# Dense experts of layer 0: the low parts of u, and of the spilled v, made by VectorE instead of GpSimd

## The chip, the cores and the metric

One core of one Trainium2 chip runs the whole program as a single launch. The metric is the device time in microseconds (us), from the start of the execution to its end. Five engines run their own queues of instructions in order: TensorE (PE; its weight loads are PEld), VectorE (DVE), ScalarE (ACT), GpSimd (POOL) and SyncE (SP), which here only issues DMA transfers.

## The reference

Two layers of a backbone, each with a token mixer and then an expert network. The change lies in the expert network of layer 0:

```python
def _peer(h, w_q, sub_k1, sub_k2, u, v):
    ...                                   # top 16 experts of each of 8 heads, of 16384: idx, gate
    def block(args):
        hb, ib, gb = args
        act = jax.nn.gelu(jnp.einsum('td,ted->te', hb, u[ib])) * gb
        return jnp.einsum('te,ted->td', act, v[ib])
```

`h` has 512 tokens of 1024 features in layer 0 (256 of context, 256 latent). `u` and `v` have 16384 rows of 1024 numbers each.

## The kernel before

The 512 tokens of layer 0 are treated in two ways. The first 128 take the **gathered** path: for each of their 128 expert places, one row of `u` and later one of `v` is fetched per token by an indirect DMA from GpSimd's queue (tile `row`, 5 buffers, 512 KB each) and used by one VectorE instruction (L1045 for a row of u, whose partial result goes to `score`; L1063 for a row of v, added to `tok`). Rows of the modulation weights (`in_w_modT`, loaded by SyncE, used by L1035) stand in the same ring. One step of the generator `gathered` (`next(work)`) uses one row and issues the fetch of the one four places on.

The other 384 tokens take the **dense** path: all 16384 experts are computed, 128 slabs of 128 experts, two slabs to a group. For a group TensorE computes the scores S = u·h (L223, 48 matmuls with 384 columns), ScalarE applies gelu into `ga` (L1108), VectorE multiplies by the gate grid (L1253), and TensorE adds the product with v into `pa` (L1306, 36 matmuls with 512 columns).

Each fp32 operand is used as a high part and a low part, so that three products stand for one. `split` makes them: ScalarE rounds the slab to the high part (`wH` of u, `vH` of v, L210), and another engine subtracts, low = raw − high (`wL`, `vL`, L214). The factor `ga` gets the parts `ah` (ScalarE, L1256) and `al` (VectorE, L1260).

18 groups (36 slabs) have their scores computed before the dense loop and are **spilled** to DRAM (`spd`); the loop first takes the 46 unspilled groups, then the 18 spilled ones, which need only their v slabs and the stored `ga`. The tables that name the engine of the low part are `LOWU` (u slabs that are spilled), `LOWV` (v slabs, one string for the unspilled and one for the spilled groups), and a literal `"g"` for the u slabs of the loop.

The order on TensorE, VectorE, ScalarE and GpSimd in this loop is that of the code (a manual schedule). In turn g the code issues the loads of v for g+1, the scores of g+1, and then the 36 matmuls of `pa` of g, in eight parts numbered d; between the parts stand: d=0 the split of u for g+2, d=1 the gating of g+1, d=4 its `al`, d=5 the split of v for g+1 (d=0 in the spilled groups), and the steps of `gathered`: one at d=0, one at d=4 and four at d=7 in the unspilled groups; one at d=5 and one at d=7 in the spilled ones. The raw slabs of u and v share one ring of four buffers (`wraw`), loaded by SyncE's queue in order. With v two slabs and u two slabs alternating, a load of u(g+2) waits for the buffers that `vL` of g has read, and a load of v waits for those that `wL` has read.

Of the kernel before, what the change touches and what calls it, by code (L numbers as in the profile page):

```python
# [66 lines left out]
SPX = ((0, 2), (0, 0))  # L67
LOWQ = ('g', 'g')
LOWU = ('g', 'g')
LOWV = (("vv", "gg"), ("vv", "vv"))  # L70
GATED = (1, 4)
VALUES = (5, 0)
USTAGE = 0
# [110 lines left out]
class Kernel:  # L184
# [891 lines left out]
    def peer(self, l, mods, todo=()):  # L1076
        nc, A, tc = self.nc, self.A, self.tc
# [9 lines left out]
        with ExitStack() as es:  # L1087
# [7 lines left out]
            def low(s):  # L1095
                return tuple({"g": "gpsimd", "v": "vector"}[x] for x in s)

            def u_load(i, spilling=False):
                return [self.w_slab(A["uT"][l, i + e], "scalar", low(LOWU[l] if spilling else "g")) for e in range(2)]

            def u_pair(ws):

# [8 lines left out]
            def spill(upto):  # L1111

                while self.spilled < min(upto, nsp):
                    i = self.spilled
                    self.spilled += 2
                    nc.sync.dma_start(sp_d[i:i + 2].rearrange("i j t -> j i t"), u_pair(u_load(i, True)))
# [93 lines left out]
            with ExitStack() as e2:  # L1210
# [13 lines left out]
                def u_stage(g):  # L1224

                    if g >= len(order):
                        return
                    i = order[g]
                    if i >= nsp:
                        b.u[g] = u_load(i)  # L1230
                    else:
                        b.ga[g] = self.t(cp, [P, 2, n], tag="ga", bufs=3)
                        nc.sync.dma_start(b.ga[g], sp_d[i:i + 2].rearrange("i j t -> j i t"))
# [28 lines left out]
                def values(g):  # L1262
                    b.vs = [self.split(vp, w, "v", 4, low={"v": "vector", "g": "gpsimd"}[LOWV[l][order[g] < nsp][e]])
                            for e, w in enumerate(b.w)]
# [197 lines left out]
```

## Time and profile before

| | before |
|---|---|
| median of 3 runs (lowest, highest) | 2970.75 us (2959.99, 2982.71) |
| the profiled execution: time, span | 2970.65 us, 2968.9 us |
| TensorE busy | 2736.3 us (92%) |
| VectorE busy | 2122.4 us (71%) |
| ScalarE busy | 1141.9 us (38%) |
| GpSimd busy | 1452.2 us (49%) |
| DMA, mean over the span | 215 GB/s |

The busy times are means over stages that have little in common. The dense loop of layer 0 runs from about 782 to 1784 us of the span, the unspilled groups to about 1635 us. Matmuls are pipelined, so a busy TensorE need not be one at its peak.

### The profile page before, as it was taken

How to read it: one execution, taken by the hardware profiler on the slowest of the kernel's cores; microseconds unless marked ns; L12 is line 12 of the kernel's file. 1: busy time of each engine (PE TensorE's matmuls, PEld its weight loads, DVE VectorE, ACT ScalarE, POOL GpSimd, SP SyncE). 2: the span in 40 equal slices, each digit the busy share in tenths (PEclk: the TensorE clock that was granted, in tenths of full speed). 3: DMA queues.
4: the chain of work that ended last, by engine and by line, in shares of the span. 5: the costliest groups of instructions: out<-in, count | busy, mean ns of one | idle time of the engine just before them, and what ended most of it. 6: DMA issues, size and time to landing. Idle time of an engine off the chain costs nothing.

```text
span 2968.9 us, 41568 instructions
## 1 busy us (share of the span) xinstructions
PE 2736.3 (92%) x15750; PEld 2417.1 (81%) x15750; DVE 2122.4 (71%) x3488; ACT 1141.9 (38%) x1742; POOL 1452.2 (49%) x779
## 2 busy tenths in 40 slices
PE   7799999889999899989998998899889999999998
PEld 4677888889988888878887776678889998887776
DVE  6894778998587787888877887846894225566665
ACT  4333343335432332323333333344344544444443
POOL 3530144455377666667765883524655665440000
PEclk9898999999999999999999998999999999999999
DMA  6321423356787878888888982423557777667784
GB/s 230 107 93 60 127 89 110 101 195 257 271 315 278 302 279 297 304 296 318 309 298 311 338 273 85 142 64 116 160 160 252 241 255 225 189 190 260 271 277 167
DMA packets 265784, 639.24 MB, mean 215 GB/s; under 512 B 19184, under 2 KB 136688, under 8 KB 262768
## 3 DMA queue, kind: packets, MB, share of 16 engines
q1 hardware_dynamic: 228720, 502.36, 50.4%
q0 software_dynamic: 36864, 134.23, 12.3%
q8 instruction: 123, 2.02, 0.3%
q14 instruction: 77, 0.63, 0.1%
HBM read 574.39 MB, written 62.13 MB: 214 GB/s over the span
## 4 chain that ended last, share of the span: by engine, by line
PE 26%; DMA 22%; DVE 22%; issue 12%; POOL 6%; ACT 3%; DVEq 0%; SPq 0%; POOLq 0%; ACTq 0%
PE S L223 10%; DMA wraw<-in_uT_dram 9%; PE mm L223 8%; DVE vL L214 5%; DMA ga<-spd 5%; PE G L1196 4%; DMA row<-in_u_dram,idx 4%; DMA row<-in_v_dram,idx 3%; DVE ga L1253 2%; POOL vL L214 2%; POOL wL L214 1%; POOL row L1012 1%; DVE t L1045 1%; ACT ah L1256 1%; PE pa L1306 1%
## 5 line engine op out<-in xcount | busy, mean ns | idle before, releaser
L214 POOL TENSOR_TENSOR wL<-wraw,wH 128x1024 fp32r<-128x1024 f32 x320 | 828.7, 2596 | 814.4 <-ACT wH L210 667.6
L223 PE MATMUL S<-hH,wL 128*128 128x384 f32 (+1 forms) x2048 | 620.7, 321 | 48.4 <-POOL wL L214 48.4
L223 PE MATMUL S<-hH,wH 128*128 128x384 f32 (+1 forms) x2048 | 619.7, 320 | 26.2 <-ACT wH L210 24.3
L210 ACT ACTIVATE wH<-wraw 128x1024 fp32r<-128x1024 f32 x320 | 336.9, 1054 | 374.8 <-DMA wraw<-in_uT_dram 342.1
L223 PEld LDWEIGHTS S<-hH,wL 128*128 128x128 f32 x2048 | 403.7, 197 | 59.7 <-POOL wL L214 57.6
L223 PEld LDWEIGHTS S<-hH,wH 128*128 128x128 f32 x2048 | 403.5, 197 | 33.6 <-ACT wH L210 29.0
L1306 PE MATMUL pa<-vH,al 128*128 128x512 f32 x1280 | 399.9, 394 | 23.0 <-DVE al L1260 22.5
L1306 PE MATMUL pa<-vH,ah 128*128 128x512 f32 x1280 | 395.5, 390 | 4.2 <-ACT ah L1256 3.5
L1306 PE MATMUL pa<-vL,ah 128*128 128x512 f32 x1280 | 395.2, 390 | 2.5 <-DVE vL L214 2.5
L223 PE MATMUL S<-hL,wH 128*128 128x384 f32 (+1 forms) x2048 | 349.9, 311 | 0.0
L214 DVE TENSOR_TENSOR vL<-wraw,vH 128x1024 fp32r<-128x1024 f32 x220 | 290.4, 1350 | 73.4 <-ACT vH L210 73.2
L1260 DVE TENSOR_TENSOR al<-ga,ah 128x768 fp32r<-128x768 f32 (+1 forms) x128 | 212.7, 1662 | 171.7 <-ACT ah L1256 171.7
L210 ACT ACTIVATE vH<-wraw 128x1024 fp32r<-128x1024 f32 x256 | 262.7, 1052 | 178.2 <-PE pa L1306 112.2
L223 PEld LDWEIGHTS S<-hL,wH 128*128 128x128 f32 x2048 | 314.8, 192 | 0.0
L1306 PEld LDWEIGHTS pa<-vH,al 128*128 128x128 f32 x1280 | 236.6, 188 | 88.3 <-DVE al L1260 41.7
L1108 ACT ACTIVATE ga<-S 128x384 f32<-128x384 f32 (+1 forms) x256 | 111.3, 435 | 464.1 <-PE S L223 463.5
L1306 PEld LDWEIGHTS pa<-vL,ah 128*128 128x128 f32 x1280 | 240.0, 188 | 54.5 <-DVE vL L214 4.0
L1306 PEld LDWEIGHTS pa<-vH,ah 128*128 128x128 f32 x1280 | 238.0, 188 | 51.5 <-ACT ah L1256 5.0
L223 PE MATMUL mm<-hH,wH 128*128 128x256 f32 (+1 forms) x776 | 257.6, 351 | 9.0 <-ACT hH L361 2.5
L223 PE MATMUL mm<-hH,wL 128*128 128x256 f32 (+1 forms) x776 | 253.0, 345 | 9.9 <-DVE wL L214 9.6
L1253 DVE TENSOR_TENSOR ga<-ga,gt 128x768 f32<-128x768 f32 (+1 forms) x128 | 165.4, 1292 | 115.0 <-DMA ga<-spd 78.5
L1012 POOL DMA_INDIRECT row<-in_v_dram,idx x128 | 190.4, 1488 | 110.5 <-DVE tok L1063 88.4
(323 smaller groups left out, 4182.6 us busy)
## 6 DMA issues: line engine op xcount, KB each, us to landing
wraw<-in_uT_dram SPq DMA_DIRECT2D x256, 512.0 KB, 4.5
wraw<-in_v_dram SPq DMA_DIRECT2D x256, 512.0 KB, 5.4
gd<-gst SPq DMA_DIRECT2D x20, 2048.0 KB, 6.7
wraw<-in_w_in_dram SPq DMA_DIRECT2D x52, 512.0 KB, 3.6
gt<-gd SPq DMA_DIRECT2D x32, 768.0 KB, 7.1
row<-in_w_modT_dram SPq DMA_DIRECT2D x48, 512.0 KB, 7.2
wraw<-in_w_modT_dram SPq DMA_DIRECT2D x32, 512.0 KB, 3.7
wraw<-in_w_q_dram SPq DMA_DIRECT2D x32, 512.0 KB, 3.7
```

The lines of the kernel that those rows point to most:

```text
L210: nc.scalar.activation(h, w, AF.Copy)
L214: e.tensor_tensor(lo, w, h.bitcast(F32), op=ALU.subtract)
L223: nc.tensor.matmul(ps, x, y, start=start and m == 0, stop=stop and m == len(seq) - 1, skip_group_check=skip)
L1012: Gp.indirect_dma_start(out=x, out_offset=None, in_=rows[n], in_offset=bass.IndirectOffsetOnAxis(ap=idx[:, k:k + 1], axis=0))
L1045: V.tensor_tensor_reduce(j, x, ht, 1.0, 0.0, op0=ALU.mult, op1=ALU.add, accum_out=a[:, k:k + 1])
L1108: self.gelu = S.activation(ga[:, e, :], ps, AF.Gelu_apprx_tanh)
L1196: nc.tensor.matmul(pg[:, t, :], Y[:, q + t, :], X[:, q + t, :], start=True, stop=True)
L1253: V.tensor_tensor(gv, gv, b.gt[:, :, g % 2 * 2:g % 2 * 2 + 2].rearrange("p b e t -> p e b t"), op=ALU.mult)
L1256: S.activation(b.ah, ga, AF.Copy)
L1260: V.tensor_tensor(b.al, b.gated, b.ah.bitcast(F32), op=ALU.subtract)
L1306: nc.tensor.matmul(pacc[tau, h], (ah, ah, al)[m][:, e, tau * P:(tau + 1) * P], vs[e][m == 1][:, h * 512:h * 512 + 512], start=g == 0 and e ...
```

## The change

The low part of the u slabs of the unspilled groups (46 x 2) goes from GpSimd to VectorE through a new table, LOWD, and so does the low part of the v slabs of the spilled groups (18 x 2), through LOWV. Layer 1 keeps what it had. In layer 0's dense loop GpSimd then holds the issues of the row fetches alone.

```diff
 LOWU = ('g', 'g')
-LOWV = (("vv", "gg"), ("vv", "vv"))
+LOWD = ("v", "g")
+LOWV = (("vv", "vv"), ("vv", "vv"))
...
             def u_load(i, spilling=False):
-                return [self.w_slab(A["uT"][l, i + e], "scalar", low(LOWU[l] if spilling else "g")) for e in range(2)]
+                return [self.w_slab(A["uT"][l, i + e], "scalar", low(LOWU[l] if spilling else LOWD[l])) for e in range(2)]
```

What that makes of the queues, at three places (lines of the changed kernel are one higher; numbers behind names are those of single buffers).

VectorE, around the gating of one unspilled group, before:

```order
L1045 ISA t_1609_8106,score_5653<-row_8018,tok_5640 128x1024
L1045 ISA score_5653 128x1
L1253 TENSOR_TENSOR ga_8036<-ga_8036,gt_7888 128x768
L1260 TENSOR_TENSOR al_8116<-ga_8036,ah_8115 128x768
L1045 ISA t_1613_8133,score_5653<-row_8022,tok_5640 128x1024
```

and in the changed kernel (the `row` step that stands first here is the one at d=0, behind four steps of the turn before):

```order
L215 TENSOR_TENSOR wL_8097<-wraw_8094,wH_8096 128x1024
L215 TENSOR_TENSOR wL_8103<-wraw_8100,wH_8102 128x1024
L1046 ISA t_1609_8106,score_5653<-row_8018,tok_5640 128x1024
L1046 ISA score_5653 128x1
L1254 TENSOR_TENSOR ga_8036<-ga_8036,gt_7888 128x768
L1261 TENSOR_TENSOR al_8116<-ga_8036,ah_8115 128x768
L1046 ISA t_1613_8133,score_5653<-row_8022,tok_5640 128x1024
```

The two subtractions of u stand ahead of the step at d=0, and so ahead of the gating of the next group.

GpSimd, at the same stage, before:

```order
L1012 DMA row_9336<-in_u_dram,idx_5139 128x1024
L214 TENSOR_TENSOR wL_9405<-wraw_9402,wH_9404 128x1024
L214 TENSOR_TENSOR wL_9411<-wraw_9408,wH_9410 128x1024
L1012 DMA row_9443<-in_u_dram,idx_5139 128x1024
L1012 DMA row_9468<-in_u_dram,idx_5139 128x1024
L1012 DMA row_9472<-in_u_dram,idx_5139 128x1024
```

and in the changed kernel:

```order
L1013 DMA row_9336<-in_u_dram,idx_5139 128x1024
L1013 DMA row_9443<-in_u_dram,idx_5139 128x1024
L1013 DMA row_9468<-in_u_dram,idx_5139 128x1024
L1013 DMA row_9472<-in_u_dram,idx_5139 128x1024
L1013 DMA row_9478<-in_u_dram,idx_5139 128x1024
L1013 DMA row_9560<-in_u_dram,idx_5139 128x1024
```

Between two fetches of rows there is no other instruction left.

VectorE, in the spilled groups, before:

```order
L1253 TENSOR_TENSOR ga_13569<-ga_13569,gt_13622 128x768
L1260 TENSOR_TENSOR al_13649<-ga_13569,ah_13648 128x768
L1063 SCALAR_TENSOR_TENSOR tok_10208<-row_13546,score_5653,tok_10208 128x1024
L1063 SCALAR_TENSOR_TENSOR tok_10208<-row_13558,score_5653,tok_10208 128x1024
L1253 TENSOR_TENSOR ga_13633<-ga_13633,gt_13622 128x768
L1260 TENSOR_TENSOR al_13710<-ga_13633,ah_13709 128x768
```

and in the changed kernel:

```order
L215 TENSOR_TENSOR vL_13636<-wraw_13624,vH_13635 128x1024
L215 TENSOR_TENSOR vL_13640<-wraw_13625,vH_13639 128x1024
L1254 TENSOR_TENSOR ga_13569<-ga_13569,gt_13622 128x768
L1261 TENSOR_TENSOR al_13649<-ga_13569,ah_13648 128x768
L1064 SCALAR_TENSOR_TENSOR tok_10208<-row_13546,score_5653,tok_10208 128x1024
L1064 SCALAR_TENSOR_TENSOR tok_10208<-row_13558,score_5653,tok_10208 128x1024
L215 TENSOR_TENSOR vL_13697<-wraw_13685,vH_13696 128x1024
L215 TENSOR_TENSOR vL_13701<-wraw_13686,vH_13700 128x1024
```

Each group begins with the two subtractions of v, ahead of its gating.

## Rows read from the trace of the kernel before

**Rows 1.** Windows of the dense part: unspilled groups, then spilled; busy us, instructions, clock, DMA.

```profile
808.00:1618.00 810.00, 748.60 (x3636) 675.99 (x3636) 647.95 (x640) 247.74 (x302) 548.31 (x303) 0.96 0.83 300
1640.00:1790.00 150.00, 141.01 (x607) 111.64 (x606) 132.79 (x83) 49.55 (x51) 126.34 (x56) 1.00 0.86 294
```

**Rows 2.** The chain of waits, 782 to 1640 us: shares by line, and its longest piece.

```profile
by line: DMA wraw<-in_uT_dram 23.7%; issue 22.7%; DMA row<-in_u_dram,idx 11.4%; DMA row<-in_v_dram,idx 9.6%; DVE ga L1253 5.8%; DVE vL L214 4.9%; DVE t L1045 4.5%; POOL wL L214 3.5%; ACT ah L1256 2.9%; POOL row L1012 2.7%; ACT wH L210 2.6%;
...
1561.94 14.22 DMA wraw<-in_uT_dram
```

**Rows 3.** DMA of 808 to 1618 us; last number of an issue: median us to landing.

```profile
DMA packets 94593, 242.74 MB, mean 300 GB/s; under 512 B 7216, under 2 KB 39472, under 8 KB 94546
...
wraw<-in_uT_dram SPq DMA_DIRECT2D x86, 512.0 KB, 7.5
```

**Rows 4.** Groups on VectorE, 808 to 1618 us: count, busy us, mean ns, idle before.

```profile
L1045 DVE CUSTOM_DVE_ANT_0 t<-row,tok 128x1024 bf16<-128x1024 f32 x118 | 171.3, 1480 | 39.3 <-DMA row<-in_u_dram,idx 39.2
...
L214 DVE TENSOR_TENSOR vL<-wraw,vH 128x1024 fp32r<-128x1024 f32 x86 | 101.2, 1217 | 0.0
...
L1253 DVE TENSOR_TENSOR ga<-ga,gt 128x768 f32<-128x768 f32 x43 | 82.5, 1919 | 0.0
...
L1260 DVE TENSOR_TENSOR al<-ga,ah 128x768 fp32r<-128x768 f32 x43 | 80.5, 1871 | 76.5 <-ACT ah L1256 76.5
```

**Rows 5.** Timeline of VectorE in one group: start, duration, then what ended its idle time.

```profile
1169.56 2.35 DVE L214 TENSOR_TENSOR vL<-wraw,vH 128x1024 fp32r<-128x1024 f32 x2
...
1174.29 1.22 DVE L1045 CUSTOM_DVE_ANT_0 t<-row,tok 128x1024 bf16<-128x1024 f32 x1
...
1182.31 3.41 DVE L1045 CUSTOM_DVE_ANT_0 t<-row,tok 128x1024 bf16<-128x1024 f32 x1
...
1185.66 0.95 DVE L1253 TENSOR_TENSOR ga<-ga,gt 128x768 f32<-128x768 f32 x1
...
1187.52 0.96 DVE L1260 TENSOR_TENSOR al<-ga,ah 128x768 fp32r<-128x768 f32 x1 [0.91 <-ACT ah L1256]
```

**Rows 6.** Timeline of GpSimd in the same group.

```profile
1169.64 1.95 POOL L1012 DMA_INDIRECT row<-in_u_dram,idx  x1 [0.30 <-DVE score L1045]
...
1171.90 0.94 POOL L1012 DMA_INDIRECT row<-in_u_dram,idx  x1 [0.30 <-issue]
...
1178.89 5.75 POOL L214 TENSOR_TENSOR wL<-wraw,wH 128x1024 fp32r<-128x1024 f32 x2 [0.18 <-ACT wH L210]
```

**Rows 7.** Timeline of the DMA queue and ScalarE in the same group.

```profile
1170.80 1.46 SPq L388 DMA_DIRECT2D wraw<-in_uT_dram  x2
...
1177.75 1.06 ACT L210 ACTIVATE wH<-wraw 128x1024 fp32r<-128x1024 f32 x1 [3.44 <-DMA wraw<-in_uT_dram]
...
1180.12 1.06 ACT L210 ACTIVATE wH<-wraw 128x1024 fp32r<-128x1024 f32 x1 [1.30 <-DMA wraw<-in_uT_dram]
...
1187.25 1.56 SPq L1247 DMA_DIRECT2D wraw<-in_v_dram  x2
```

**Rows 8.** Timeline of TensorE in the same group, at the full clock.

```profile
1172.06 1.40 PEld L223 LDWEIGHTS S<-hL,wH 128*128 128x128 f32 x8
...
1174.53 0.62 PE L1306 MATMUL pa<-vH,al 128*128 128x512 f32 x2
...
1174.98 0.61 PE L1306 MATMUL pa<-vH,ah 128*128 128x512 f32 x2
```

**Rows 9.** Timeline of a short group: DMA queue, VectorE, ScalarE, and VectorE again.

```profile
1460.79 3.67 SPq L1247 DMA_DIRECT2D wraw<-in_v_dram  x2
...
1469.04 2.35 DVE L214 TENSOR_TENSOR vL<-wraw,vH 128x1024 fp32r<-128x1024 f32 x2
...
1476.36 1.06 ACT L210 ACTIVATE wH<-wraw 128x1024 fp32r<-128x1024 f32 x1 [0.29 <-DMA wraw<-in_uT_dram]
...
1484.99 2.35 DVE L214 TENSOR_TENSOR vL<-wraw,vH 128x1024 fp32r<-128x1024 f32 x2
```

**Rows 10.** The residual of the factors on VectorE in the spilled groups, 1650 to 1780 us.

```profile
L1260 DVE TENSOR_TENSOR al<-ga,ah 128x768 fp32r<-128x768 f32 x15 | 47.0, 3136 | 14.4 <-ACT ah L1256 14.4
```

## The prediction, made before the changed kernel was run

> **What bounds the kernel now.** I looked first at the windows of the dense loop [rows 1]. In the 810 us of unspilled groups TensorE is busy for 748.6 us at a mean granted clock of 0.96, VectorE for 648, GpSimd for 548, and the DMA engines for 0.83 of the time. Nothing is full, so I asked what a group takes and what it could take. The 86 `vL` of that window [rows 4] are 43 groups, so a group lasts 810 / 43 = 18.84 us. TensorE alone: eight score matmuls are loaded in 1.40 us, 0.175 each, and two value matmuls follow two others after 0.45 us, 0.225 each [rows 8]; 48 x 0.175 + 36 x 0.225 = 16.5 us. DMA alone: 242.74 MB [rows 3] / 43 = 5.65 MB a group; 300 GB/s at a share of 0.83 is 361 GB/s at a share of 1, so 15.6 us. VectorE alone: 648 / 43 = 15.1 us. A group is 2.3 us longer than the longest of these. It is bound by a chain, not by an engine.
>
> The chain of waits says which [rows 2]: its largest named part, 23.7%, is the transfer of u. The timeline of one group shows the loop. VectorE starts the two `vL` at 1169.56 [rows 5]; the first gives a buffer free, and at 1170.80 SyncE issues the loads of u; ScalarE begins the second `wH` when its slab has landed, at 1180.12 [rows 7]; `ah` stands behind it on ScalarE, `al` behind `ah`, then a row step, then the next two `vL`. I call the time from the start of a `vL` pair to the start of the second `wH` W1. Here it is 10.56 us. I read it in all 43 groups: 7.3 us in the shortest [rows 9], 16.7 in the longest (2.35 and 14.22 us, [rows 2]), 11.1 in the mean.
>
> The second thing to see is the price of the subtractions on GpSimd beside VectorE. One row step takes 1.22 us, another 3.41 us [rows 5], and the second one lies within the 5.75 us in which GpSimd made two `wL` [rows 6]. `ga` and `al` take 0.95 and 0.96 us when alone [rows 5], and 1.92 and 1.87 in the mean [rows 4].
>
> **The change part by part.**
>
> *Collisions removed.* Per group on VectorE: `ga` 1.92 - 0.95 = 0.97, `al` 1.87 - 0.96 = 0.91, and row steps of u (1.48 - 1.22) x 118 / 43 = 0.71; 2.6 us together [rows 4, 5]. The steps of other kinds gain too, and I leave them out. The Trainium skill (page "SBUF — State Buffer", section "Who interferes with whom") has it that a VectorE instruction with two SBUF inputs and a GpSimd instruction that reads SBUF exclude each other for their whole length. By that rule, with two subtractions of about 2.4 us in a group, up to 4.8 us would go, against the 2.6 of the rows; the sum uses the rows.
>
> *Subtractions added.* Two `wL` on VectorE, priced as the two `vL` beside them: 2.35 us a group [rows 5]. VectorE's work becomes 15.1 - 2.6 + 2.35 = 14.9 us a group, so it isn't overloaded.
>
> *The wait that is added.* `wL` of u(g+2) now stands in VectorE's queue and waits for `wH`, so for u's transfer. Behind it are queued a row step, `ga` and `al` of the next group, another step, and its two `vL`; for those wait TensorE and the next load of u. Much of this wait is there already, since `al` waits for `ah`, which is behind `wH` on ScalarE: 76.5 us in 43 groups [rows 4]. The new loop is, from the start of a `vL` pair: W1, then `wH` 1.06 [rows 7], hand-over 0.1, the second `wL` 1.18, a row step 1.22, `ga` 0.95, `ah` with its hand-over 0.91, `al` 0.96, a row step 1.22 [rows 5]; 7.6 us, with the short readings of accumulators between them 7.7. A group takes W1 + 7.7. With the mean W1 of today, 11.1, that is 18.8 us: no change. **All depends on W1.**
>
> *What becomes of W1.* It consists of 1.24 us to the issue, some 1.1 us to the second issue and a transfer whose median is 7.5 us [rows 3, 7]; the spread from 7.3 to 16.7 us is competition on the DMA engines. In the short group the two loads of v before it went out at 1460.79 (done within 3.67 us), 8.2 and about 4.6 us ahead of the `vL` at 1469.04; W1 was 7.3 us and the group 15.95 us [rows 9]. In the ordinary group of rows 7 the loads of v went out at 1187.25, 7.1 us after the second `wH`, because GpSimd's 5.75 us stood between. After the change v is released by `wL` on VectorE: the first load some 5.4 us, or with the first slab 7.7 us, ahead of the next `vL` in every group (7.7 less 2.3 for the second `wH` and `wL`; the first `wH` is 2.4 us earlier [rows 7]). That is close to the short group, so more of v will have landed when u is asked for. Bounds: 7.3 us, and 11.1 as now or somewhat over it. I take 9.7, between the two and nearer the mean, since the ordinary group also has four row fetches in its way: 9.7 + 7.7 = **17.4 us a group**. TensorE's 16.5, DMA's 15.6 and VectorE's 14.9 plus about 0.9 for `ah` all lie under it. Rate of DMA: 5.65 / 17.4 = 325 GB/s, 0.90 of 361. For 45 turns of the unspilled part (46 groups): 45 x (18.84 - 17.4) = **65 us less**.
>
> *Row fetches.* GpSimd has five or six issues of 0.94 to 1.95 us [rows 6] and nothing else, so it idles for half of a group. A row asked for after the step at d=0 is used in the fourth step behind the next `vL`, some 10 us on; it can be late by a little, but behind that step VectorE waits for `wH` anyway. Nothing counted.
>
> *Spilled groups.* 607 matmuls in 150 us [rows 1] make 8.9 us for 36. TensorE's floor is 36 x 0.225 = 8.1, DMA's 294 x 8.9 / 361 = 7.2. GpSimd's two `vL` go, and `al`, now 3.1 us [rows 10], falls to 0.96. VectorE gets 2.35 (`vL`) + 0.95 + 0.91 + 0.96 + two row steps of about 1.3 = 7.8 us: just under TensorE. Between 8.1 and 8.9 I take 8.5: 18 x 0.4 = **7 us less**. If the collisions stayed, VectorE would need 10 us and the part would be 20 us longer; with GpSimd's subtractions gone there is nothing to collide with.
>
> *Ends of the loop.* The first u pairs and the last v pair move to VectorE too; a pair is 2.35 us on either side of zero. Nothing counted.
>
> Sum against the profiled execution (2970.65 us; the median of the runs is 2970.75): 2970.65 - 65 - 7 = **2899 us**.
>
> **The rivals.**
>
> *TensorE becomes the bound.* If W1 comes down to 8.8 or less, TensorE's 16.5 us hold. For it: groups of 15.95 us exist [rows 9]. Against it: at 16.5 us DMA would have to move 342 GB/s, 0.95 of its rate, all the time. 45 x 2.34 + 18 x 0.8 = 120 us less: 2851 us.
>
> *No change.* W1 stays at 10.4 to 11.1 us, because u's transfer is slowed by rows and not by v. The group takes 18.1 to 18.8 us: 0 to 33 us less, and 0 to 7 in the spilled part: 2931 to 2971 us.
>
> *Slower: u queues behind rows, at the head of VectorE's queue.* The four row steps behind `vL` let four fetches go, just when u is asked for. Today one or more of them wait until GpSimd is through with `wL`; then they won't. Each row of 0.52 MB that is served ahead of u costs 0.52 / 361 = 1.45 us. Two more of them make W1 9.7 + 2.9 = 12.6 and a group 20.3 us: 45 x 1.46 - 7 = 59 us more, 3030 us. It decides from W1 = 11.1 on. Against it: the short groups also had their four row steps at once.
>
> *Issues of rows are held up by VectorE.* One issue took 1.95 us beside two `vL`, another 0.94 us [rows 6]. With two more subtractions in the queue each late issue costs 1.0 us, and where the row of the fourth step is the one, up to 1.4 us a group wouldn't be hidden: 45 x 1.4 = 63 us of the gain are lost, 2962 us. The same section of the Trainium skill names this: descriptors of GpSimd's DMAs wait while VectorE holds the shared port; but it excepts `tensor_tensor`, which is what is added here, and the 1.95 us speak against that exception.
>
> **How the numbers follow.** Forecast (2875 to 2930) 0.50; TensorE's floor 0.17; no change 0.18; slower 0.12; held-up issues 0.03. A measurement of this kernel can tell about 1%, 30 us, from no change. Faster by more: the first two and the upper edge of the third, 0.70; within 1%: 0.18; slower by more: 0.12. The range reaches from TensorE's floor over no change to a W1 a little above today's: 2850 to 2985 us.
>
> **What the changed profile would show.** `ga` and `al` at 0.95 to 1.0 us and L1045 near 1.23 us in the mean; `wL` on VectorE with an idle time before it of some 1 to 2 us a group that ends with ScalarE's `wH`; loads of v issued at once behind `wL`; u's median to landing below 7.5 us; DMA at about 325 GB/s; 43 groups in about 750 us, and spilled groups of about 8.5 us. If W1 has not fallen, the step on v's earlier loads is wrong; if `ga` and `al` are still near 1.9 us, the step on collisions is.

## The result, and the profile after

| | before | after |
|---|---|---|
| median (lowest, highest; runs) | 2969.81 us (2959.99, 2982.71; 4) | 2889.51 us (2884.87, 2898.09; 4) |
| ratio | | 0.9749, 95% interval 0.9707 to 0.979 |
| span of the profiled execution | 2968.9 us | 2891.8 us |
| 45 unspilled groups, first to 46th `ga` (gating, L1253; L1254 after) | 836.3 us | 765.5 us |
| 18 spilled groups, 46th to last `ga` | 155.9 us | 151.0 us |
| group length: unspilled (43, from the third `ga` on), spilled | 18.69, 8.66 us | 17.06, 8.39 us |
| W1, mean (lowest, highest) | 11.1 (7.3, 16.7) us | 9.5 (7.3, 12.8) us |

The changed kernel is 2.5% faster; 2899 us were forecast. Of the 77.1 us between the two spans, 70.8 lie in the unspilled groups, 4.9 in the spilled ones and 1.5 ahead of the loop; behind it 0.2 us were added. The last two are no result: in the profiles of all the runs below, which change hardly anything outside the loop, its first `ga` starts between 781.6 and 798.4 us, and the stretch behind its last `ga` takes 1175.6 to 1194.0 us.

The windows of the dense loop after, unspilled and spilled groups, to be held against [rows 1] (us, then busy time of PE, PEld, DVE, ACT and POOL, granted clock as a share of the full 2.4 GHz, DMA share, GB/s):

```profile
808.00:1540.00 732.00, 719.60 (x3604) 645.78 (x3602) 607.46 (x721) 243.34 (x298) 309.81 (x215) 1.00 0.92 329
1566.00:1700.00 134.00, 132.21 (x587) 108.89 (x586) 108.53 (x113) 48.06 (x49) 33.83 (x21) 1.00 0.94 334
```

TensorE is now busy for 0.98 of the unspilled stretch at a mean granted clock of 1.00, where it was 0.92 at 0.96; VectorE is at 0.83, and the DMA engines have gone from 0.83 to 0.92 of the time. The groups of VectorE in the same stretch, which answer to [rows 4]:

```profile
L1046 DVE CUSTOM_DVE_ANT_0 t<-row,tok 128x1024 bf16<-128x1024 f32 x118 | 140.0, 1221 | 0.0
...
L215 DVE TENSOR_TENSOR wL<-wraw,wH 128x1024 fp32r<-128x1024 f32 x85 | 103.5, 1225 | 81.9 <-ACT wH L211 81.3
...
L215 DVE TENSOR_TENSOR vL<-wraw,vH 128x1024 fp32r<-128x1024 f32 x86 | 101.3, 1220 | 0.0
...
L1261 DVE TENSOR_TENSOR al<-ga,ah 128x768 fp32r<-128x768 f32 x42 | 40.3, 959 | 40.9 <-ACT ah L1257 40.9
...
L1254 DVE TENSOR_TENSOR ga<-ga,gt 128x768 f32<-128x768 f32 x42 | 40.0, 953 | 0.0
```

`ga`, `al` and the row steps have the durations that they had when alone: 0.95, 0.96 and 1.22 us in the mean, from 1.92, 1.87 and 1.48. The wait for rows of u, 39.3 us, is gone, and the wait for `ah` has halved. In their place stands the wait of `wL` for ScalarE's `wH`, 81.9 us for 85 subtractions, 1.9 us a group. The chain of waits and its longest piece, against [rows 2]:

```profile
by line: DMA wraw<-in_uT_dram 35.7%; issue 20.2%; DVE vL L215 11.1%; ACT wH L211 5.1%; DVE ga L1254 5.0%; ACT ah L1257 4.7%; DVE t L1046 4.7%; DVE t L1036 3.7%; DVE tok L1064 3.6%; DVE wL L215 2.6%; PE S L224 2.1%; DMA wraw<-in_v_dram 0.5%;
...
878.58 10.32 DMA wraw<-in_uT_dram
```

The transfer of u is still the largest part, now 35.7%; nothing of GpSimd is left among the named parts. The transfers, against [rows 3]:

```profile
DMA packets 95075, 240.84 MB, mean 329 GB/s; under 512 B 7150, under 2 KB 40561, under 8 KB 95029
...
wraw<-in_uT_dram SPq DMA_DIRECT2D x86, 512.0 KB, 6.4
...
wraw<-in_v_dram SPq DMA_DIRECT2D x84, 512.0 KB, 6.1
...
gt<-gd SPq DMA_DIRECT2D x21, 768.0 KB, 9.5
```

u lands in 6.4 us (median) after 7.5. In the timelines of 42 groups, the second load of u is issued 2.38 us after the start of the `vL` pair in both kernels, and takes 8.7 us to land before and 7.0 after (means): the fall of W1 is the fall of this transfer and nothing else. `gt`, the slab of the gate grid, is loaded for every second group; its part in W1 is told further below.

One group of the timeline shows the loop that the prediction wrote down (VectorE, the DMA queue and ScalarE, in the order of the loop):

```profile
1152.50 2.36 DVE L215 TENSOR_TENSOR vL<-wraw,vH 128x1024 fp32r<-128x1024 f32 x2
...
1153.75 1.46 SPq L389 DMA_DIRECT2D wraw<-in_uT_dram  x2
...
1161.58 1.06 ACT L211 ACTIVATE wH<-wraw 128x1024 fp32r<-128x1024 f32 x1 [0.29 <-DMA wraw<-in_uT_dram]
...
1161.33 2.57 DVE L215 TENSOR_TENSOR wL<-wraw,wH 128x1024 fp32r<-128x1024 f32 x2 [1.89 <-ACT wH L211]
...
1162.58 1.67 SPq L1248 DMA_DIRECT2D wraw<-in_v_dram  x2
...
1166.23 0.95 DVE L1254 TENSOR_TENSOR ga<-ga,gt 128x768 f32<-128x768 f32 x1
...
1168.15 0.96 DVE L1261 TENSOR_TENSOR al<-ga,ah 128x768 fp32r<-128x768 f32 x1 [0.97 <-ACT ah L1257]
...
1170.17 2.36 DVE L215 TENSOR_TENSOR vL<-wraw,vH 128x1024 fp32r<-128x1024 f32 x2
```

From the `vL` pair at 1152.50 to the second `wH` at 1161.58 are 9.1 us, W1; v's loads go out at 1162.58, as soon as the first `wL` has let a buffer go, and 7.6 us ahead of the next `vL` at 1170.17.

GpSimd's row fetches around a `vL` pair have moved too. Before (`vL` at 1169.56, [rows 5]), one fetch stood behind the two `wL` and went out at 1168.30, and another began at 1169.64 [rows 6], both ahead of u's loads at 1170.80 [rows 7]:

```profile
1162.92 4.76 POOL L214 TENSOR_TENSOR wL<-wraw,wH 128x1024 fp32r<-128x1024 f32 x2 [2.57 <-ACT wH L210]
...
1168.30 1.04 POOL L1012 DMA_INDIRECT row<-in_u_dram,idx  x1 [0.62 <-issue]
```

After (`vL` at 1170.17), one is left there, and the one before it went out 8.4 us ahead of the `vL`:

```profile
1161.78 1.57 POOL L1013 DMA_INDIRECT row<-in_u_dram,idx  x1 [0.30 <-issue]
...
1170.53 1.67 POOL L1013 DMA_INDIRECT row<-in_u_dram,idx  x1 [7.17 <-DVE score L1046]
```

Counted over 42 groups from 3 us ahead of the `vL` pair to 1.3 us behind its start, when u is asked for, it is 1.8 row fetches a group before and 0.8 after.

### The profile page after: what moved, and what is told of

Its sections match the earlier page's. It is cut to its first block, busy times and chain, and to the rows that moved or that the text cites. A ratio compares the mean times of both kernels' runs of the same rounds, so it can differ in the third digit from the quotient of the medians.

```text
span 2891.8 us, 41509 instructions
## 1 busy us (share of the span) xinstructions
PE 2716.0 (94%) x15750; PEld 2398.9 (83%) x15750; DVE 2072.2 (72%) x3616; ACT 1142.5 (40%) x1742; POOL 1102.7 (38%) x651
## 4 chain that ended last, share of the span: by engine, by line
PE 32%; DVE 25%; DMA 18%; issue 9%; ACT 4%; POOL 2%; DVEq 0%; ACTq 0%; POOLq 0%; SPq 0%
DMA wraw<-in_uT_dram 12%; PE S L224 11%; PE mm L224 8%; DVE vL L215 7%; DMA ga<-spd 5%; PE pa L1307 5%; PE G L1197 5%; ACT ah L1257 2%; DVE ga L1254 2%; ACT wH L211 2%; DVE t L1046 1%; DVE wL L215 1%; DVE eq L939 1%; DVE al L1261 1%; DVE tok L1064 1%
## 5 line engine op out<-in xcount | busy, mean ns | idle before, releaser
L215 POOL TENSOR_TENSOR wL<-wraw,wH 128x1024 fp32r<-128x1024 f32 x228 | 577.3, 2535 | 739.7 <-ACT wH L211 542.7
L224 PE MATMUL S<-hH,wL 128*128 128x384 f32 (+1 forms) x2048 | 606.2, 314 | 20.6 <-POOL wL L215 13.3
L224 PE MATMUL S<-hH,wH 128*128 128x384 f32 (+1 forms) x2048 | 605.7, 314 | 5.0 <-ACT wH L211 3.2
L224 PEld LDWEIGHTS S<-hH,wL 128*128 128x128 f32 x2048 | 393.4, 192 | 31.1 <-POOL wL L215 14.5
L224 PEld LDWEIGHTS S<-hH,wH 128*128 128x128 f32 x2048 | 393.1, 192 | 10.6 <-ACT wH L211 5.7
L215 DVE TENSOR_TENSOR vL<-wraw,vH 128x1024 fp32r<-128x1024 f32 x256 | 333.3, 1332 | 66.1 <-ACT vH L211 64.8
L1013 POOL DMA_INDIRECT row<-in_u_dram,idx x128 | 180.9, 1413 | 270.6 <-DVE score L1046 230.0
L1261 DVE TENSOR_TENSOR al<-ga,ah 128x768 fp32r<-128x768 f32 (+1 forms) x128 | 137.4, 1074 | 138.0 <-ACT ah L1257 138.0
```

What stands on the lines that cost most here:

```text
L215: e.tensor_tensor(lo, w, h.bitcast(F32), op=ALU.subtract)
L224: nc.tensor.matmul(ps, x, y, start=start and m == 0, stop=stop and m == len(seq) - 1, skip_group_check=skip)
L1013: Gp.indirect_dma_start(out=x, out_offset=None, in_=rows[n], in_offset=bass.IndirectOffsetOnAxis(ap=idx[:, k:k + 1], axis=0))
L1261: V.tensor_tensor(b.al, b.gated, b.ah.bitcast(F32), op=ALU.subtract)
```

## The experiments

Group lengths and W1 are read as in the table above, from the timeline of each run's profile. Ratios are against the kernel before, on the same chip.

| run | median, us | ratio, 95% interval | unspilled, us | spilled, us | W1, us |
|---|---|---|---|---|---|
| u_only | 2896.2 | 0.976 (0.9694 to 0.9825) | 16.98 | 8.65 | 9.4 |
| v_only | 2957.1 | 0.9946 (0.9916 to 0.9975) | 18.67 | 8.32 | 11.1 |
| hold | 2945.5 | 0.9915 (0.9883 to 0.9947) | 18.25 | 8.60 | 10.5 |
| before_ring | 2956.8 | 0.9981 (0.9949 to 1.0013) | 17.84 | 9.57 | 3.7 |
| after_ring | 2872.2 | 0.967 (0.9612 to 0.9728) | 16.39 | 8.47 | 8.6 |
| fill | 2913.3 | 0.9799 (0.9736 to 0.9861) | 17.69 | 8.59 | 10.1 |
| shadow | 2975.4 | 1.0001 (0.9965 to 1.0036) | 19.09 | 8.53 | 8.6 |
| hold_fill | 3002.5 | 1.0094 (1.0048 to 1.0141) | 19.83 | 8.61 | 12.1 |
| after_t2 | 2903.1 | 0.9762 (0.9735 to 0.979) | 17.18 | 8.49 | 9.6 |
| after_again | 2887.7 | 0.9702 (0.9675 to 0.9729) | 16.94 | 8.37 | 9.4 |
| ring_again | 2867.0 | 0.9634 (0.9613 to 0.9655) | 16.39 | 8.47 | 8.6 |

Three theories stood against each other. *Chain*: a group lasts W1 + 7.7 us, and W1 falls because v's loads go out earlier. *Collisions*: VectorE's own instructions got shorter. *Queue*: row fetches no longer stand behind subtractions in GpSimd's queue.

**u_only: the u subtractions alone.**

```diff
-LOWV = (("vv", "vv"), ("vv", "vv"))
+LOWV = (("vv", "gg"), ("vv", "vv"))
```

> Only the u subtractions move to VectorE; the two v subtractions of a spilled group stay on GpSimd. Chain theory (a group lasts W1 + 7.7 us, and W1 falls since v's loads go out earlier): the unspilled groups keep the whole fall from 18.7 to 17.1 us, the spilled ones stay at 8.7 us, so 5 us more than the changed kernel, about 2895 us. Collision theory (VectorE's work per group is what shrank): the same sign, and the spilled part, where each group has collisions too, must be as much worse as theirs cost, 18 x 2 us = 36 us more, about 2925 us.

The unspilled groups keep the whole gain; the spilled ones stay at 8.65 us. That the span is that of the changed kernel, 2891.8 us, is chance: the 4.8 us more in the spilled groups are made up for by the scatter of the other stages. The residual of the factors in the spilled groups (`al` on VectorE, 1560 to 1690 us) is as long as in [rows 10]:

```profile
L1261 DVE TENSOR_TENSOR al<-ga,ah 128x768 fp32r<-128x768 f32 x14 | 45.3, 3236 | 14.1 <-ACT ah L1257 14.1
```

**v_only: the v subtractions of the spilled groups alone.**

```diff
-LOWD = ("v", "g")
+LOWD = ("g", "g")
```

> Only the v subtractions of the spilled groups move. Chain theory: there is no W1 in the spilled groups, TensorE's 8.1 us are near: 5 us less than before, about 2965 us. Collision theory: al and ga lose some 3 us a group, 18 groups, up to 40 us less, about 2930 us.

Windows of the spilled groups, and `al` in them (1650 to 1780 us):

```profile
1640.00:1790.00 150.00, 148.41 (x657) 122.06 (x656) 122.84 (x124) 51.15 (x52) 41.84 (x24) 1.00 0.91 320
...
L1261 DVE TENSOR_TENSOR al<-ga,ah 128x768 fp32r<-128x768 f32 x16 | 15.3, 958 | 15.4 <-ACT ah L1257 15.4
```

`al` falls from 3.1 to 0.96 us, yet a group only from 8.66 to 8.32 us, because TensorE, busy for 148 of 150 us at full clock, is the bound. The 18 groups are 6.1 us shorter, the unspilled ones as long as before; the medians differ by 12 us (7 to 25 by the interval of the ratio), and nothing in the loop accounts for the rest. In the spilled part nearly all of what the collisions cost VectorE, some 3 us a group, was time that nobody waited for. That refutes the collision theory there, and the u part carries nearly all of the change.

**hold: v's loads held back, by tiny reads on VectorE.**

```diff
+        self.raws = (getattr(self, "raws", []) + [w])[-2:]
...
-                        b.u[g] = u_load(i)
+                        b.u[g], b.raws = u_load(i), list(self.raws)
...
                             gated_low(g + 1)
+                            if not last and g + 2 in b.u:
+                                for w in b.raws:
+                                    x = self.t(cp, [P, 8], tag="held", bufs=1)
+                                    V.tensor_copy(x, w[:, 0, :8])
```

`b.raws` holds the two raw u slabs of g + 2.

> The changed kernel, with two tiny copies (128x8) on VectorE behind al that read the raw u slabs of the group after next, so that the buffers are released, and v's loads issued, some 5 us later; nothing else is moved, no work on GpSimd. Chain theory: v's loads end their issue right before the next vL pair, W1 goes back to 11 to 12 us, a group to 19 to 20 us: 90 to 130 us more than the changed kernel, 2980 to 3020 us. Collision theory and queue theory (row fetches no longer wait behind subtractions on GpSimd): only the copies cost, 0.3 us a group, about 2905 us.

The reads, the loads of v that they release, and the next `vL` pair, in the timeline:

```profile
1166.24 0.37 DVE L1303 COPY held<-wraw 128x8 f32<-128x8 f32 x2
...
1166.47 0.81 SPq L1249 DMA_DIRECT2D wraw<-in_v_dram  x2
...
1168.93 2.35 DVE L215 TENSOR_TENSOR vL<-wraw,vH 128x1024 fp32r<-128x1024 f32 x2
```

The issue of v's loads now ends 0.4 us (mean of 42 groups) ahead of the next `vL`; in the changed kernel it ended 4.9 us ahead, in the kernel before 1.7. W1 rises by 1.0 us and a group by 1.2, with as many row fetches ahead of u (0.8 a group) as in the changed kernel and u's loads issued as early after `vL`: the time at which v's loads go out does set W1. But it rises less than I expected, and W1 stays below the 11.1 us of the kernel before although v goes out later than there. The chain theory is right in its mechanism and not the whole.

**before_ring: two raw buffers of their own for v, on the kernel before.**

```diff
-b.w = [self.t(None, [P, KT, P], tag="wraw").rearrange("p k n -> p (k n)") for e in range(2)]
+b.w = [(self.t(None, [P, KT, P], tag="wraw") if last else self.t(vp, [P, KT, P], tag="vraw", bufs=2)).rearrange("p k n -> p (k n)") for e in range(2)]
...
-            for tag, bufs in (..., ("t2", 4), ...):
+            for tag, bufs in (..., ("t2", 3), ...):
```

> The kernel before, with two raw buffers of their own for v in layer 0's dense loop, so that a load of u no longer waits for vL and a load of v no longer for wL (to make room, the ring of scratch tiles t2 has three buffers in place of four). All subtractions are where they were, with all collisions. Chain theory: W1 is no longer in the loop, a group falls from 18.7 to about 17 us: about 75 us less than before, 2895 us. Collision theory and queue theory: VectorE and GpSimd do what they did, the group stays near 18.7 us, about 2970 us.

Windows of the unspilled groups, `ga` and `al` there, and the split of v on ScalarE in the spilled part (1600 to 1750 us):

```profile
808.00:1540.00 732.00, 694.94 (x3465) 626.18 (x3465) 656.28 (x615) 224.69 (x285) 522.78 (x290) 0.99 0.88 316
...
L1253 DVE TENSOR_TENSOR ga<-ga,gt 128x768 f32<-128x768 f32 x40 | 75.0, 1875 | 0.0
...
L1260 DVE TENSOR_TENSOR al<-ga,ah 128x768 fp32r<-128x768 f32 x40 | 68.7, 1717 | 36.5 <-ACT ah L1256 36.5
...
L210 ACT ACTIVATE vH<-vraw 128x1024 fp32r<-128x1024 f32 x31 | 32.9, 1061 | 109.1 <-DMA vraw<-in_v_dram 109.1
```

u's transfer has left the loop (W1 3.7 us), and the unspilled groups gain 0.85 us, not 1.7: they stay at 17.84. Neither theory had said so. The collisions are all there (`ga` 1.88, `al` 1.72 us), and so is GpSimd's queue; one of them, or both, holds the group once u doesn't; which, this run doesn't show. In the spilled part my edit left v with two buffers in place of four, ScalarE waits 109 us for v, and of the 40.5 us that the unspilled groups gain 16.4 are lost there.

**after_ring: the ring on the changed kernel, in the unspilled groups only.**

```diff
+own = not last and i >= nsp
-b.w = [self.t(None, [P, KT, P], tag="wraw").rearrange("p k n -> p (k n)") for e in range(2)]
+b.w = [(self.t(vp, [P, KT, P], tag="vraw", bufs=2) if own else self.t(None, [P, KT, P], tag="wraw")).rearrange("p k n -> p (k n)") for e in range(2)]
...
-            for tag, bufs in (..., ("t2", 4), ...):
+            for tag, bufs in (..., ("t2", 3), ...):
```

> The changed kernel, with two raw buffers of their own for v in the unspilled groups of layer 0, so that loads of u and v no longer wait for each other's buffers (t2 with three buffers in place of four, to make room). The kernel before with such a ring kept 17.8 us a group, although W1 had left its loop. If that rest was the collisions (VectorE held beside GpSimd's subtractions), it isn't here, and TensorE's 16.5 us a group are the bound: about 25 us less than the changed kernel, 2865 us. If a group of 17.1 us is held by something else (rows of the gathered path, DMA rate), it stays near 2890 us.

```profile
808.00:1540.00 732.00, 732.00 (x3720) 668.01 (x3719) 632.37 (x745) 252.08 (x313) 327.00 (x222) 1.00 0.96 343
```

The chain of waits, 850 to 1500 us:

```profile
by line: PE S L224 50.5%; PE pa L1308 49.5%
```

TensorE is busy for the whole window (732 of 732 us), the chain is its two kinds of matmuls and nothing else, most groups last 16.5 us to the tenth, and the DMA engines move 343 GB/s at a share of 0.96. With neither u in the loop nor subtractions on GpSimd, TensorE is the bound. Against before_ring, where only the place of the subtractions differs in these groups, they are 1.45 us shorter. So GpSimd's subtractions, by collisions or in its queue, cost that much a group even where u's transfer holds nothing.

**fill: GpSimd's queue held by work that hardly reads SBUF**, behind each pair of u slabs in the dense loop of layer 0.

```diff
+for wh, _ in ws:
+    x = self.t(cp, [P, KT, P], tag="shadow", bufs=1)
+    Gp.tensor_tensor(x[:, 0, :8], wh[:, 0, :8].bitcast(F32), wh[:, 0, :8].bitcast(F32), op=ALU.subtract)
+    Gp.memset(x, 0.0)
+    Gp.memset(x, 0.0)
```

> The changed kernel, with work for GpSimd that reads next to nothing: per u slab a subtraction of 8 columns, which waits for wH as wL did, and two memsets of a 128x1024 scratch tile. So GpSimd's queue, with the row fetches in it, is held behind the transfer of u and then for some us, as before, and no long read of SBUF collides with VectorE. Queue theory (rows came late behind the subtractions): a group goes back towards 18.7 us, about 2950 us. Collision and chain theories: nothing waits for it, within 10 us of the changed kernel.

Row steps of u and `wL` on VectorE, the memsets (one of two lines) and the short subtractions on GpSimd, 808 to 1540 us:

```profile
L1046 DVE CUSTOM_DVE_ANT_0 t<-row,tok 128x1024 bf16<-128x1024 f32 x117 | 140.1, 1221 | 24.7 <-DMA row<-in_u_dram,idx 24.7
...
L215 DVE TENSOR_TENSOR wL<-wraw,wH 128x1024 fp32r<-128x1024 f32 x82 | 99.7, 1224 | 60.6 <-ACT wH L211 60.2
...
L1106 POOL MEMSET shadow<- 128x1024 f32 x82 | 78.4, 957 | 4.7
...
L1104 POOL TENSOR_TENSOR shadow<-wH 128x8 f32<-128x8 f32 x82 | 58.6, 715 | 48.5 <-ACT wH L211 45.3
```

VectorE's durations don't move (1.221 and 1.224 us): of the 82 `wL`, 47 ran at least 0.5 us beside a memset, and the longest of these took 1.24 us. Rows come late: 24.7 us of waiting ahead of the row steps of u, where the changed kernel has none. That isn't what lengthens the group, for the wait of `wL` behind them is shorter by nearly as much (60.6 us after 81.9). W1 rises by 0.6 us to 10.1, and so does the group, 17.06 to 17.69. v's loads go out as early as in the changed kernel (4.9 us ahead), but 2.1 row fetches a group, in place of 0.8, now go out just ahead of u. Queue theory: GpSimd's queue does cost some 0.6 us a group, and not by rows that come late but by rows that are fetched in front of u.

**shadow: the same with a whole subtraction.**

```diff
-    Gp.tensor_tensor(x[:, 0, :8], wh[:, 0, :8].bitcast(F32), wh[:, 0, :8].bitcast(F32), op=ALU.subtract)
-    Gp.memset(x, 0.0)
-    Gp.memset(x, 0.0)
+    Gp.tensor_tensor(x, wh.bitcast(F32), wh.bitcast(F32), op=ALU.subtract)
```

> As the run with memsets, but GpSimd makes a whole subtraction of 128x1024 per u slab (wH less wH, into a scratch tile that nobody reads): the same wait, the same length as wL had, and two SBUF inputs. The difference from the run with memsets is the collisions alone. Collision theory: ga, al and the row steps go back to means of 1.9 and 1.5 us, and wL, which now starts together with the subtraction, is held too, so that v's loads go out later: 1.5 to 3 us a group, 2960 to 3020 us. Queue theory: the same as the run with memsets.

```profile
L1046 DVE CUSTOM_DVE_ANT_0 t<-row,tok 128x1024 bf16<-128x1024 f32 x118 | 167.0, 1449 | 0.0
...
L215 DVE TENSOR_TENSOR wL<-wraw,wH 128x1024 fp32r<-128x1024 f32 x76 | 145.9, 1929 | 36.2 <-ACT wH L211 35.6
...
L1104 POOL TENSOR_TENSOR shadow<-wH 128x1024 f32<-128x1024 f32 x76 | 189.1, 2488 | 15.8 <-ACT wH L211 12.5
```

Here `wL` is 1.93 us in the mean and the row steps 1.45; `ga` and `al`, which come after the subtraction has ended, stay at 0.99 and 0.96, other than expected. A group is 1.4 us longer than in fill. W1 is short, 8.6 us, and the rest of the loop 10.6 in place of 7.7: the collisions lengthen the part behind W1. They don't hit the instructions that they hit in the kernel before (`ga`, `al`, row steps), but `wL` above all: the 59 that meet a subtraction take 2.13 us, the 15 that meet none 1.22. The Trainium skill (page "SBUF — State Buffer", section "Who interferes with whom") says that an instruction of VectorE with two SBUF inputs contends with one of GpSimd that reads SBUF and not with one that only writes it; this pair of runs agrees, with 1.93 us for `wL` beside reads and 1.22 beside memsets.

**hold_fill: both holds at once.**

> Both at once on the changed kernel: v's loads held back (as in the run with tiny copies, which took W1 from 9.5 to 10.5 us) and GpSimd's queue held by memsets (W1 10.1 us), still without collisions. If W1 is made up of the two causes side by side, it is 9.5 + 1.0 + 0.6 = 11.1 us, as in the kernel before, and a group 11.1 + 7.9 = 19.0 us, about 2975 us. If the two causes are one and the same, W1 stays near 10.5 us and a group near 18.3, about 2945 us.

`wL` on VectorE, 808 to 1540 us:

```profile
L215 DVE TENSOR_TENSOR wL<-wraw,wH 128x1024 fp32r<-128x1024 f32 x72 | 88.0, 1225 | 123.0 <-ACT wH L211 122.7
```

W1 is 12.1 us and a group 19.8, more than the sum of the two. Late loads of v and bunched row fetches seem to make each other worse, as both end up in front of u; that reason is argued and not shown. `wL` waits 3.4 us a group for `wH`. They are two causes, but not simply additive ones.

**after_t2, after_again and ring_again: is the ring the gain?**

> The changed kernel with three scratch tiles t2 in place of four, the side edit of the runs with a ring for v. Those tiles are only written by VectorE in the dense loop, so nothing there should wait for one: the time of the changed kernel, within 10 us. If it is faster, that much of the ring's gain isn't the ring's.

> The changed kernel once more, beside the one with the ring on the same chip: about 2890 us.

> The changed kernel with the ring for v once more: its unspilled groups ran at 16.4 us, TensorE's floor, against 17.1, so 30 us less than the changed kernel on the same chip, about 2860 us; no less than 20 if the ring is what did it.

Three scratch tiles make nothing faster: an unspilled group takes 17.18 us, against 16.94 and 17.06 in two profiles of the changed kernel, and the median is 15 us above that of the changed kernel beside it, where less than 10 were expected; whether the fourth tile is worth that much stays open, as the two intervals all but touch. On the same chip the kernel with the ring takes 2867.0 us against 2887.7, with intervals that don't touch (0.9613 to 0.9655, 0.9675 to 0.9729): 21 us, where 30 were expected and at least 20. Against after_t2, which differs from it in the ring alone, it is 36 us. The kernel with the ring is the fastest of these kernels, 3.7% below the kernel before.

## Why the prediction was right, point by point

*The loop.* "A group takes W1 + 7.7" holds: from `vL` to `vL`, 42 groups last 17.20 us in the mean, a W1 of 9.49 and a rest of 7.71 (from `ga` to `ga` the table has 17.06). *W1*: 9.7 was taken, 9.5 came. That it came so close is in part luck: 9.7 was chosen between two bounds and not worked out, and of the fall from 11.1 not all is v's. The run nearest to v's earlier loads alone is fill, where the row fetches still go out in front of u: its W1 of 10.1 would make, in the prediction's sum, a group of 17.8 and 47 us less in place of 65. *Unspilled part*: 65 us forecast, 70.8 measured; the 18.84 us of before, counted from the `vL` in a window, are 18.69 from `ga` to `ga`, and the new length was 17.06 and not 17.4. *Spilled part*: 7 us forecast, 4.9 measured. The 8.9 us of before, counted from the matmuls in a window, are 8.66; TensorE was already near its bound there (v_only: 8.32 us a group at best), and 8.5 was about right. *Ends of the loop*: counted at nothing; the 1.5 us ahead of the loop are within the scatter of that stage.

*Collisions.* They went as forecast, instruction by instruction. VectorE's work fell from 15.0 to 14.2 us a group (`ga` to `ga`); 14.9 had been forecast, as the gains of the steps of v and of the modulation rows were left out. But the loop's rest behind W1 is 7.7 us before and after, and the whole fall lies in W1, so the shortening isn't VectorE's work. What the collisions did to the loop is their size in another place. Without them the two added subtractions fit into the same 7.7 us behind W1; with them (shadow) the rest becomes 10.6 us and the whole gain is lost.

*What lowers W1* is the step whose reason was only partly right. The prediction gave all of it to v's earlier loads, and for the row fetches said "nothing counted". hold shows that v's loads do it: some 4.5 us later make W1 1.0 us longer. fill shows that GpSimd's queue does it too: 0.6 us with v's loads as early as ever. In the kernel before, row fetches stood behind `wL`, and 1.8 a group went out just ahead of u; in the changed kernel it is 0.8. So the fall of 1.6 us has both causes. How much each had in the kernel before stays open, since the two together gave more than their sum.

*What the short group was.* The prediction put the spread of W1 from 7.3 to 16.7 us down to competition on the DMA engines, and read its short group as one whose loads of v went out early. Another load has as large a part: every second group has the load of `gt`, 768 KB, in flight beside u, as a rule issued 3 to 4 us ahead of the `vL` pair. With it W1 is 10.9 us in the mean in the changed kernel, without it 8.1; before, 12.5 and 9.8. The short group of [rows 9] is one without it and the longest, 16.7 us, one with it, so a part of what was read from them as v's is `gt`'s. Both kinds of groups fell by 1.6 to 1.7 us, and the account of the fall stands; moving `gt`'s load was not tried.

*The rivals.* "Slower: u queues behind rows" had the sign reversed: GpSimd's subtractions didn't keep fetches out of u's way, they pushed them into it (1.8 fetches just ahead of u against 0.8). "TensorE becomes the bound" didn't come about, but the argument against it was wrong: after_ring moves 343 GB/s, 0.96 of the time, through the whole stretch. What held the changed kernel above 16.5 us were the buffers that loads of u and v take from each other. "Issues of rows are held up by VectorE" cost nothing: VectorE's wait for rows of u is 0.0 us in the changed kernel.

## What to carry to other kernels

Before an instruction is moved to another engine, write down the loop that closes over a shared ring of buffers: which read frees which load, and what waits for that load. Here loads of u and v freed each other, and the time of every group was that of one transfer plus a fixed chain; the move helped because the reads that free v's buffers came earlier and because DMA issues no longer stood behind subtractions in GpSimd's queue, not because an engine had less to do, and two buffers more for v did 21 us more. An instruction on a second engine isn't free if it reads SBUF while the first engine's two-input instructions run, nor if DMA issues stand behind it in its queue; a filler that only writes tells the two apart.

## What the runs showed of the hardware that was not expected

Two 128x1024 fp32 memsets on GpSimd (0.96 us each) beside VectorE's subtractions cost VectorE nothing (fill: 1.224 us), a subtraction of the same shape makes them 1.93 us (shadow). A row fetch takes GpSimd 0.94 us to issue while VectorE is idle (12 fetches of the changed kernel, 808 to 1540 us) and 1.68 us beside its two `vL` (35 fetches); nothing waited for the difference. In after_ring the DMA engines held 343 GB/s at a share of 0.96 over 732 us with the row fetches of GpSimd's queue among them, where the kernel before had 300 at 0.83. And the granted clock of TensorE, 0.96 in the unspilled groups before, is 1.00 after: between 808 and 1540 us the kernel before has 11 stretches at the lower level, 1.2 GHz, 61 us in all, and the changed kernel one of 3.4 us. Where the waits between groups are longest (hold_fill, 19.8 us a group) it is 0.95, and where TensorE never waits (after_ring) 1.00.
